# Where the pre-added weight sums of a Strassen-like feed-forward group begin, and when ScalarE splits its last lent operands

## Chip, cores, metric

The kernel runs on one core of a Trainium2 chip. The metric is device time in microseconds (us): the median of several executions. Engines: PE (TensorE), DVE (VectorE), ACT (ScalarE), POOL (GpSimd) and SP, which here only issues DMAs.

## The reference

One layer of a backbone on 640 tokens (128 context, 512 latent), width 1024: a half-step SwiGLU feed-forward block, a mixer (bidirectional chunked mLSTM beside a gated convolution), a second feed-forward block and a last norm, all in float32. What matters here is the second feed-forward block:

```python
D_MODEL, D_FF = 1024, 2816
def swiglu(h, w1, w2):
    a, b = jnp.split(h @ w1, 2, axis=-1)
    return (jax.nn.silu(a) * b) @ w2
...
    h = modulate(rmsnorm(x, norm_g[2]), sh2, sc2)
    x = x + 0.5 * g2[:, None, :] * swiglu(h, ffn2_w1, ffn2_w2)
...
y_prompt, y_sample = rmsnorm(xp, final_norm), rmsnorm(xs, final_norm)
```

## The kernel before

**Numbers.** Every float32 operand x is split into hi (rounded to the fp32r type; a ScalarE cast, line 75) and lo = x - hi (a VectorE subtraction, line 79). A product of two operands is three matmuls into the same accumulator: hi times hi, hi times lo, lo times hi (lines 288 to 290). Weight tiles are 128 x 512, hi named `wh`, lo named `wl`; the moving operand is 128 x 320, half of the 640 tokens.

**Pairs.** Work comes in pairs of 128-column weight tiles over 1024 rows (`pair_el`). A pair is computed as a 2 x 2 block product with seven block products instead of eight (a Strassen-Winograd form). In order: A11, S1, S2, A12, S3, S4, A22. S1 = A21 + A22, S2 = S1 - A11, S3 = A11 - A21 and S4 = A12 - S2 are sums of weight blocks (the code only adds; the signs go into the other operand and the last sums). Their partners are sums of the moving operand's blocks, in sets of four hi/lo tiles called 11, T1, T2, 21, T3, 22, T4 in the same order. A block product is 12 matmuls, a pair 84. PSUM tiles: `a` takes A11, is copied to `b` by ScalarE (line 332) and then takes A12; `b` takes S2, is copied to `c` by ScalarE (line 347, negated) and then takes S4; `c` takes S3 and A22. So the S3 product can't start before the copy of b to c is done. The steps are numbered 0 to 6, and a dictionary `at` names small functions that are emitted right behind a step; whatever is emitted earlier stands earlier in its engine's queue, and every engine works its queue in order.

**Weight sums.** In a pair that isn't `summed`, SP loads two 512 KB tiles (`wr`, line 218), and VectorE forms S1 to S4 into `ws` tiles (line 270; 128 x 512). In a `summed` pair, S1 and S3 come from the DMA: SP loads two 256 KB quarters into one `wr` tile, POOL issues two 256 KB loads that accumulate onto them (line 235), SP loads a 512 KB `wr` tile and a 256 KB `wq` tile. VectorE then makes only S2 and S4. `wr` has five buffers, `wq` one; the loads are issued in the program's order, as buffers come free, and the weight casts run four block products ahead of PE.

**Groups.** The second feed-forward block (`ffn` with groups 8, 8, 6) goes through the 2816 hidden columns in two groups of eight tiles (`eights`) and one plain group of six. The first two tiles of the first group are done elsewhere (`n_head` = 2). A group of eight has w1 pairs 0 to 7 (silu(a) times b, 1024 hidden columns in all), then four w2 pairs (m = 0, 2, 4, 6; the first of them `summed`) that multiply the result back to width 1024. In the w2 pairs the hidden activations take the place of the moving operand, again in seven sets: five in tiles of their own, T3 and T4 in tiles lent from the block's input. For that the input's T3 and T4 were stored to DRAM (`hd`); in the last w2 pair, behind steps 4 and 6, `h_back` has POOL issue eight loads each that bring them back (tiles `HT3h`, `HT3l`, `HT4h`, `HT4l`, line 1042). Behind step 4 of the next group's first pair, `x_end` has POOL issue the last two accumulating writes of the group's result to DRAM (`xd`, line 1030; the others were issued in the w2 pairs).

**Deferred steps.** The evaluations of a pair put the splits and subtractions that make the hidden sets into a list `lazy`: for pairs 0 to 3 three entries (split for set 11; a subtraction; split for T1), for pairs 4 to 7 three entries (T2; 21 and the last subtraction for T3; 22 and the addition for T4). They are filled behind step 0 of the next pair at the earliest. `relax` empties the list, `relax_some(n)` takes n entries. The second group's pairs empty it behind step 1 (`pops`); the first w2 pair empties it behind step 0, and then splits the last tile of T3 and the four of T4 (`put_lent`) behind steps 1 to 3.

Of the kernel before, what the change touches and what calls it, by code (L numbers as in the profile page):

```python
# [44 lines left out]
def mixer_step(ctx: ExitStack, tc: tile.TileContext, x_prompt, x_sample, state_C, state_n, state_m,  # L45
# [23 lines left out]
    def t3():  # L69
        return tp.tile([P, HT], F32, name="t3", bufs=8)  # L70
# [3 lines left out]
    def split(raw, hi, lo, owe=False):  # L74
        A.copy(hi, raw)  # L75
        if owe:
            owed.append(lambda: V.tensor_sub(lo, raw, f32(hi)))
        else:
            V.tensor_sub(lo, raw, f32(hi))  # L79
# [136 lines left out]
    def w_load(w, row0, nk, col0, ncol):  # L216
        def load(t):
            nc.sync.dma_start(t[:, :nk * P].rearrange("p (k n) -> p k n", k=nk),
                              dap(w, row0 * ncol + col0, [[ncol, P], [P * ncol, nk], [1, P]]))
        load.src = (w, row0, col0, ncol)  # L220
        return load
# [81 lines left out]
    def joined(a, b):  # L303
        return {i: [*a.get(i, ()), *b.get(i, ())] for i in {*a, *b}}

    def relax_some(n):
        for _ in range(min(n, len(lazy))):
            lazy.pop(0)()
# [66 lines left out]
    def pair_el(load1, load2, ev, e1=None, spare_v=False, acts=HB, at=None, calm=False, gated=None,  # L375
                summed=False):
        po = pair_ops(summed, e1)
        at = at or {}

        def emit():  # L380
            nf = len(fill)
            for i, _ in enumerate(pair_steps(ORDER, ev, spare_v, acts, gated)):
                if not calm:
                    relax(7 - i if i else 9)
                drain(nf - nf * (i + 1) // 7)
                for f in at.get(i, ()):
                    f()
        return dict(element(pair_loads(load1, load2, summed), [po[name] for name in ORDER], emit), pair=True)
# [91 lines left out]
    def blocks_of(p):  # L480
        return [(p[i], lambda h, ps, i=i: p[2](i, h, ps)) for i in range(2)]
# [86 lines left out]
    at = 0  # L568
# [288 lines left out]
    def upair():  # L857
        return (PO["u"].tile([P, HT], F32R, name="Uh", bufs=PO["un"]),
                PO["u"].tile([P, HT], F32R, name="Ul", bufs=PO["un"]))
# [4 lines left out]
    def hpair(o):  # L864
        return (hpool(o).tile([P, HT], F32R, name="H" + o + "h", bufs=4),
                hpool(o).tile([P, HT], F32R, name="H" + o + "l", bufs=4))
# [162 lines left out]
    def x_add(m, y):  # L1029
        G.dma_start(xd[m], y, accum_op=OP.add)  # L1030
# [7 lines left out]
    def h_back(o):  # L1038
        for k in range(4):
            HB[o][k] = hpair(o)  # L1040
            for i in range(2):
                G.dma_start(HB[o][k][i], hd[o, k, i])

    def eights(w1, w2, g, f0, n_head, head, more, back):

        spare = (*range(n_head, n_head + 4), 7) if f0 < n_head else (7,)
        UB = {o: [None] * 4 for o in OPS_H}

        def tile_of(m):
            if "xs" not in PO:  # L1050
                PO["xs"] = [xp.tile([P, T], (F32, F32R)[i // 4], name="x", bufs=KT) for i in range(KT)]
            return PO["xs"][m]
        slot = lambda a, k: tile_of(2 * a + k // 2)[:, hsl(k % 2)]
        raw3 = lambda k: slot(0, k)
        raw2 = lambda k: slot(1, k)

        def put_own(o, k, src):
            UB[o][k] = hl = upair()
            split(src, *hl)

        def put_22(k, src):
            UB["22"][k] = hl = [tile_of(4 + k)[:, hsl(i)] for i in range(2)]
            split(src, *hl)

        def put_lent(o, k, src):
            UB[o][k] = hl = hpair(o)
            split(src, *hl)

        def ev_of(j):
            sa, k = {}, j % 4  # L1070

            left = [lambda: put_own("11", k, sa[0])]
            diff_1 = [lambda: V.tensor_sub(raw2(k), raw3(k), sa[0]), lambda: put_own("T1", k, raw2(k))]

            def t2():
                V.tensor_sub(raw2(k), raw2(k), sa[1])
                put_own("T2", k, raw2(k))

            def t3_():
                put_own("21", k, sa[0])  # L1080
                V.tensor_sub(raw3(k), raw3(k), sa[1])

            def t4():
                put_22(k, sa[1])
                V.tensor_add(raw2(k), sa[0], raw2(k))
            diff_2 = [t2, t3_, t4]

            def ev(mi, h, src):
                if mi == 0:
                    sa[h] = raw3(k) if h and j < 4 else t3()  # L1090
                    A.activation(sa[h], src, AF.Silu)
                    return
                V.tensor_mul(sa[h], src, sa[h])
                if j < 4:
                    lazy.extend(diff_1 if h else left)
                elif h:
                    lazy.extend(diff_2)
            return ev
        grp = []
        for j in range(8):  # L1100
            p = (w_load(w1, 0, KT, (f0 + j) * P, 2 * DFF), w_load(w1, 0, KT, DFF + (f0 + j) * P, 2 * DFF), ev_of(j))
            at = {}
            if j == 7:
                lent = lambda k: lambda: put_lent("T3", k, raw3(k))
                at = {4: [lent(0), lent(1), lent(2)], 6: [flush]}
            due = j - n_head if f0 < n_head else 8
            if due:
                pops = {1: (3, 2, 1), 2: (2, 2, 2), 3: (3, 2)}.get(due, (8,))
                at = joined(at, {i + 1: [lambda n=n: relax_some(n)] for i, n in enumerate(pops)})
            if f0 + j < n_head:  # L1110
                head.extend(blocks_of(p))
            else:
                grp.append(pair_el(*p, at=joined(at, more.get(j, {})), spare_v=j in spare, calm=True,
                                   summed=j > 1))
        w2s = []
        PO["x_end"] = []
        for m in range(0, KT, 2):
            rows_ = lambda i, m=m: (tile_of((m + i) % 4), modT[:, g, m + i, 0:1])

            def ev(mi, h, src, m=m):  # L1120
                y = tile_of((m + mi) % 4)
                if h and m == KT - 2:
                    PO["x_end"].append(lambda: x_add(m + mi, y))
                    return
                if h:
                    x_add(m + mi, y)
                    return
                for a, b, cd in ((0, P, 1), (P, HT, 0)):
                    A.activation(y[:, a:b], src[:, a:b], AF.Copy, scale=modT[:, g, m + mi, cd:cd + 1])
            at = {}  # L1130
            if m == 0:
                four = lambda k: lambda: put_lent("T4", k, raw2(k))
                at = {0: [relax], 1: [lambda: put_lent("T3", 3, raw3(3)), four(0)], 2: [four(1)], 3: [four(2), four(3)]}
            elif m == KT - 2 and back:
                at = {4: [lambda: h_back("T3")], 6: [lambda: h_back("T4")]}
            w2s.append(pair_el(w_load(w2, f0 * P, 8, m * P, D), w_load(w2, f0 * P, 8, (m + 1) * P, D), ev,
                               acts=UB, at=at, gated=rows_, spare_v=m == 0, summed=m == 0))
        return grp, w2s

    def ffn(w1, w2, g, lists, head_of, n_head, e1=None, groups=(6, 6, 6, 4), more={}):  # L1140

        head, els, f0 = [], [], 0
        for gi, size in enumerate(groups):
            if size == 8:
                els.append(eights(w1, w2, g, f0, n_head, head, more.get(gi, {}), True))
                f0 += size
                continue
# [373 lines left out]
    def hsl(h):  # L1521
        return slice(*HALVES[h])
# [717 lines left out]
```

## Time and profile before

| What | us |
|---|---|
| median of 3 runs (lowest, highest) | 1654.85 (1653.64, 1657.85) |
| the profiled execution | 1655.89 |
| its span, first to last instruction | 1654.1 |
| PE busy in it | 1632.4 (99%) |
| DVE, ACT, POOL busy | 1281.4, 837.7, 257.0 |
| mean granted PE clock | 0.997 |

A row of a timeline gives start and duration in us, engine, line, operation, output<-input, and in brackets how long the engine had been idle before it and who ended that idle time. A row of waits gives the total, the number and the longest wait. "x<-y" uses the program's tile names, with buffer numbers left out. A DMA row of POOL is its issue; the time to landing is in the DMA view.

In the profiled execution, the second group's pair 0 begins at 1366.12, its pair 1 at 1384.71, pair 2 at about 1397.9. The first group's w2 pairs begin at 1315.55, the second group's at 1471.79.

### The profile page before, as it was taken

To read this page: it belongs to the slowest core of one execution; us is meant where nothing else is said; L and a number is where in the kernel's file an instruction comes from. 1 tells how busy PE (TensorE), PEld (TensorE's weight loads), DVE (VectorE), ACT (ScalarE), POOL (GpSimd) and SP (SyncE) were. 2 spreads that over 40 slices of the span, in tenths; PEclk is the share of its full clock that TensorE was granted. 3 is DMA by queue.
4 is the path that set the end of the run, shared out by engine and by line. 5 is a ranking of instruction groups with operands and counts; after the bars stand their busy time and mean duration, and the time that the engine had idled before them with its cause. 6 is when DMAs were issued, how large, how long until landed. Compare 5 with 4: busy or idle time off the path is not lost.

```text
span 1654.1 us, 29490 instructions
## 1 busy us (share of the span) xinstructions
PE 1632.4 (99%) x11093; PEld 1587.9 (96%) x11093; DVE 1281.4 (77%) x2710; ACT 837.7 (51%) x1841; POOL 257.0 (16%) x366
## 2 busy tenths in 40 slices
PE   8999999999999999999999999999999999999998
PEld 5999999999999999999999999999999998999997
DVE  6867877887778878788897788779688875786765
ACT  5642542543566655465561455632376664565543
POOL 2010000000031322121121222011123113213002
PEclk9999999999999999999999999999999999999999
DMA  9454343343353433342358333457378767768522
GB/s 322 114 164 120 106 126 112 103 128 92 113 179 93 113 89 91 85 119 68 93 184 255 106 90 80 114 170 220 107 185 194 162 127 149 159 139 195 168 80 64
DMA packets 305806, 222.46 MB, mean 134 GB/s; under 512 B 9971, under 2 KB 282746, under 8 KB 305664
## 3 DMA queue, kind: packets, MB, share of 16 engines
q1 hardware_dynamic: 270768, 162.03, 34.4%
q0 software_dynamic: 34864, 58.54, 15.3%
q8 instruction: 87, 1.43, 0.4%
q14 instruction: 55, 0.45, 0.1%
q10 hardware_dynamic: 32, 0.01, 0.0%
HBM read 194.75 MB, written 25.79 MB: 133 GB/s over the span
## 4 chain that ended last, share of the span: by engine, by line
PE 88%; ACT 3%; DVE 3%; DMA 3%; issue 1%; POOL 0%; SPq 0%; ACTq 0%; DVEq 0%; POOLq 0%
PE ps L288 27%; PE ps L289 27%; PE ps L290 27%; PE ax L1779 2%; PE ax L1810 2%; DMA wr<-in_ffn_w_dram 1%; PE ax L1782 1%; DVE wl L79 1%; ACT Uh L931 1%; ACT wh L75 1%; DMA early<-in_w_mod_dram 1%; PE ax L1756 1%; DMA xd<-x 0%; DMA HT3l<-hd 0%; DMA x<-rd 0%
## 5 line engine op out<-in xcount | busy, mean ns | idle before, releaser
L79 DVE TENSOR_TENSOR wl<-wr,wh 128x512 fp32r<-128x512 f32 (+1 forms) x403 | 273.8, 690 | 87.9 <-ACT wh L75 85.4
L75 ACT CAST wh<-wr 128x512 fp32r<-128x512 f32 (+1 forms) x405 | 236.8, 598 | 90.9 <-PE ps L289 72.7
L79 DVE TENSOR_TENSOR wl<-ws,wh 128x512 fp32r<-128x512 f32 x296 | 204.6, 691 | 57.4 <-ACT wh L75 56.7
L75 ACT CAST wh<-ws 128x512 fp32r<-128x512 f32 x296 | 181.2, 620 | 97.2 <-DVE ws L270 72.3
L288 PE MATMUL ps<-Uh,wh 128*128 128x320 f32 x576 | 179.6, 312 | 0.0
L289 PE MATMUL ps<-Ul,wh 128*128 128x320 f32 x576 | 177.9, 309 | 0.0
L290 PE MATMUL ps<-Uh,wl 128*128 128x320 f32 x576 | 177.7, 309 | 0.0
L288 PE MATMUL ps<-HT4h,wh 128*128 128x320 f32 x408 | 128.4, 315 | 0.0
L289 PE MATMUL ps<-HT4l,wh 128*128 128x320 f32 x408 | 126.2, 309 | 0.1
L290 PE MATMUL ps<-HT4h,wl 128*128 128x320 f32 x408 | 126.1, 309 | 0.0
L288 PE MATMUL ps<-H11h,wh 128*128 128x320 f32 x376 | 118.8, 316 | 0.5 <-ACT H11h L75 0.5
L288 PE MATMUL ps<-H21h,wh 128*128 128x320 f32 x376 | 117.7, 313 | 0.0
L289 PE MATMUL ps<-H11l,wh 128*128 128x320 f32 x376 | 116.5, 310 | 0.3
L290 PE MATMUL ps<-H21h,wl 128*128 128x320 f32 x376 | 116.3, 309 | 0.0
L290 PE MATMUL ps<-H11h,wl 128*128 128x320 f32 x376 | 116.1, 309 | 0.0
L289 PE MATMUL ps<-H21l,wh 128*128 128x320 f32 x376 | 116.1, 309 | 0.0
L288 PE MATMUL ps<-HT3h,wh 128*128 128x320 f32 x356 | 112.3, 316 | 3.8 <-ACT ps L347 2.2
L289 PE MATMUL ps<-HT3l,wh 128*128 128x320 f32 x356 | 110.7, 311 | 1.1 <-DMA HT3l<-hd 1.1
L290 PE MATMUL ps<-HT3h,wl 128*128 128x320 f32 x356 | 110.2, 309 | 0.0
L288 PEld LDWEIGHTS ps<-Uh,wh 128*128 128x128 f32 x576 | 108.1, 188 | 1.2 <-issue 0.8
L289 PEld LDWEIGHTS ps<-Ul,wh 128*128 128x128 f32 x576 | 108.1, 188 | 0.4 <-DVE Ul L79 0.4
L288 PE MATMUL ps<-H22h,wh 128*128 128x320 f32 x344 | 108.1, 314 | 0.0
(483 smaller groups left out, 4733.5 us busy)
## 6 DMA issues: line engine op xcount, KB each, us to landing
wr<-in_ffn_w_dram SPq DMA_DIRECT2D x88, 512.0 KB, 4.9
wr<-in_w_in_dram SPq DMA_DIRECT2D x72, 512.0 KB, 3.9
wr<-in_w_mod_dram SPq DMA_DIRECT2D x51, 512.0 KB, 4.0
wr<-in_ffn_w_dram SPq DMA_DIRECT2D x32, 384.0 KB, 3.4
wr<-in_ffn_w_dram SPq DMA_DIRECT2D x40, 256.0 KB, 4.4
xd<-x POOLq DMA_DIRECT2D x32, 320.0 KB, 5.9
wr<-in_ffn_w_dram POOLq DMA_DIRECT2D x28, 256.0 KB, 5.0
early<-in_w_mod_dram SPq DMA_DIRECT2D x13, 512.0 KB, 8.8
```

Of the source, the lines that this page charges most:

```text
L75: A.copy(hi, raw)
L79: V.tensor_sub(lo, raw, f32(hi))
L288: PE.matmul(ps, hi[:, ws], ah, start=start, stop=False, skip_group_check=True)
L289: PE.matmul(ps, hi[:, ws], al, start=False, stop=False, skip_group_check=True)
L290: PE.matmul(ps, lo[:, ws], ah, start=False, stop=stop, skip_group_check=True)
L931: A.activation(t[:, a:b], t[:, a:b], AF.Identity, scale=sc_, bias=bi_)
L1756: PE.matmul(p[:, :P], S["k", dt][:, sl], S["q", dt][:, sl], start=(dt == 0), stop=(dt == 1))
L1779: PE.matmul(p2[:, :DH + 1], S["q", dt][:, sl], S["C"][d][:, dt, :], start=(dt == 0), stop=(dt == 1))
L1782: PE.matmul(p1[:, :DH + 1], S["p", ch][:, d, :], PO["vt"][:, ch, :], start=True, stop=True)
L1810: PE.matmul(p[:, :DH + 1], kw[:, dt * P:(dt + 1) * P], PO["vt"][:, ch, :], start=True, stop=True)
```

## The change

Three edits in `eights`. First, in the second group (`f0` = 8, not below `n_head`) the pairs are `summed` from pair 4 on, not from pair 2; the first group stays as it was. Second, in pairs 0 to 4 of the second group only two of the deferred entries are taken behind step 1, the rest behind step 2, that is, behind ScalarE's copy of b to c in program order. Third, in the first w2 pair of both groups, two deferred entries are taken behind step 0, the rest behind step 1, and the splits for T3 and T4 are each emitted one step later.

```diff
             if due:
-                pops = {1: (3, 2, 1), 2: (2, 2, 2), 3: (3, 2)}.get(due, (8,))
+                pops = {1: (3, 2, 1), 2: (2, 2, 2), 3: (3, 2)}.get(due, (2, 8) if j < 5 else (8,))
                 at = joined(at, {i + 1: [lambda n=n: relax_some(n)] for i, n in enumerate(pops)})
             if f0 + j < n_head:
                 head.extend(blocks_of(p))
             else:
                 grp.append(pair_el(*p, at=joined(at, more.get(j, {})), spare_v=j in spare, calm=True,
-                                   summed=j > 1))
+                                   summed=j > (1 if f0 < n_head else 3)))
...
             if m == 0:
                 four = lambda k: lambda: put_lent("T4", k, raw2(k))
-                at = {0: [relax], 1: [lambda: put_lent("T3", 3, raw3(3)), four(0)], 2: [four(1)], 3: [four(2), four(3)]}
+                at = {0: [lambda: relax_some(2)], 1: [relax], 2: [lambda: put_lent("T3", 3, raw3(3)), four(0)],
+                      3: [four(1), four(2)], 4: [four(3)]}
```

## The prediction

> **What bounds the kernel now.** I read the page first, then the waits of the tensor engine in the stretch that the change touches (the second feed-forward block), then the busy times of single stages, then the timeline of the two or three places where the stages were too long. The page:
>
> ```profile
> span 1654.1 us, 29490 instructions
> PE 1632.4 (99%) x11093; PEld 1587.9 (96%) x11093; DVE 1281.4 (77%) x2710; ACT 837.7 (51%) x1841; POOL 257.0 (16%) x366
> ```
>
> PE is the bound, so only time in which PE waits, or issues slowly, can be won. Its waits between 1226 and 1560 us:
>
> ```profile
> PE ps L288 <- ACT ps L347: 2.2, 3, 0.8
> PE ps L288 <- DMA HT3h<-hd: 1.7, 4, 1.1
> PE ps L289 <- DMA HT3l<-hd: 1.1, 4, 0.4
> ```
>
> Three waits for ScalarE's copy of b to c (L347), eight for the T3 set that comes back from DRAM (hd). What they cost altogether is seen better in the stages, each one pair of column tiles with 84 matmuls:
>
> ```profile
> core 0: us, PE busy (x) PEld busy (x) DVE busy (x) ACT busy (x) POOL busy (x), PEclk, DMA share, GB/s
> 1315.55:1328.90 13.35, 12.57 (x85) 12.06 (x84) 11.94 (x26) 10.15 (x24) 0.00 (x0) 1.00 0.51 138
> 1366.12:1384.71 18.59, 15.82 (x86) 13.82 (x85) 7.63 (x14) 6.30 (x15) 12.45 (x21) 0.91 1.16 249
> 1384.71:1397.90 13.19, 12.61 (x87) 12.34 (x86) 8.90 (x17) 6.50 (x15) 1.59 (x2) 1.00 0.68 118
> 1397.90:1410.20 12.30, 12.30 (x85) 12.30 (x85) 8.81 (x17) 6.55 (x15) 0.56 (x1) 1.00 0.31 87
> 1471.79:1485.10 13.31, 12.52 (x84) 12.09 (x83) 11.82 (x25) 10.23 (x24) 0.00 (x0) 1.00 0.51 138
> 1521.00:1533.30 12.30, 12.30 (x86) 12.30 (x85) 8.01 (x14) 5.49 (x12) 10.25 (x19) 1.00 1.16 273
> ```
>
> The rows are: first w2 pair of the first group of eight; pairs 0, 1 and 2 of the second group; first w2 pair of the second group; first pair of the last group of six. An undisturbed pair takes 12.30 us, or 0.1465 us a matmul. Four of these stages are longer, by 1.05, 6.29, 0.89 and 1.01 us: 9.24 us, all that the touched stretch has to give.
>
> **The long stage.** PE and POOL in pair 0 of the second group, and the same place one group later:
>
> ```profile
> 1373.01 0.31 PE L290 MATMUL ps<-H21h,wl 128*128 128x320 f32 x1
> 1374.45 0.38 PE L288 MATMUL ps<-HT3h,wh 128*128 128x320 f32 x1 [1.13 <-DMA HT3h<-hd]
> ...
> 1380.09 0.47 PE L288 MATMUL ps<-H22h,wh 128*128 128x320 f32 x1
> ```
> ```profile
> 1364.58 2.63 POOL L235 DMA_DIRECT2D wr<-in_ffn_w_dram  x2 [6.60 <-DVE wl L79]
> 1366.10 1.68 POOL L1042 DMA_DIRECT2D HT3h<-hd  x1
> ...
> 1373.39 0.53 POOL L1042 DMA_DIRECT2D HT3l<-hd  x1 [2.41 <-DMA wr<-in_ffn_w_dram]
> ...
> 1381.18 1.31 POOL L235 DMA_DIRECT2D wr<-in_ffn_w_dram  x1 [1.03 <-DVE t L360]
> ...
> 1517.99 0.56 POOL L1042 DMA_DIRECT2D HT3h<-hd  x1 [3.77 <-PE ps L290]
> ...
> 1526.38 0.54 POOL L1042 DMA_DIRECT2D HT4l<-hd  x1
> ```
>
> Issues and median time to landing, from 1355 to 1390 us and then from 1505 to 1545:
>
> ```profile
> HT3h<-hd POOLq DMA_DIRECT2D x4, 160.0 KB, 8.6
> HT3l<-hd POOLq DMA_DIRECT2D x4, 160.0 KB, 8.5
> HT4h<-hd POOLq DMA_DIRECT2D x4, 160.0 KB, 5.6
> ```
> ```profile
> HT3l<-hd POOLq DMA_DIRECT2D x4, 160.0 KB, 4.1
> HT4h<-hd POOLq DMA_DIRECT2D x4, 160.0 KB, 6.1
> HT4l<-hd POOLq DMA_DIRECT2D x4, 160.0 KB, 6.2
> ```
>
>  In the second group two accumulating weight loads (pair 2's) stand in POOL's queue ahead of the 16 loads that bring T3 and T4 back. The first T3 load goes at 1366.10, each takes about 8.6 us to land, and the eighth waits 2.41 us for an accumulating load to land; it goes at 1373.39, when PE wants T3 at 1373.01 + 0.15 = 1373.16. The product on T3 ends at 1380.09 in place of 1374.92: 5.17 us. The other 1.12 us of the 6.29 are lost in the matmuls that follow, which go slower (0.47 us each in place of 0.31 at 1380.09; PEclk 0.91 for the stage). One group later no accumulating load is near. The stages lie 156.24 us apart, so 1517.99 stands for 1361.75, which is 4.35 us earlier than 1366.10; T3 lands in about 4 us, and the row of 1521.00 shows no loss.
>
> **The change part by part.** (1) Pairs 2 and 3 of the second group lose four accumulating loads on POOL (1.3 us of POOL each); SP issues two 512 KB loads a pair in place of four smaller ones. POOL's next accumulating loads are pair 4's, behind the two xd writes that follow T4. The 16 loads then see what they see in the last group. T3: last of eight issued near 1365.4, landed by 1369.5; needed from 1373.16. T4: last issued near 1370.1 (1526.38 - 156.24), landed by 1376.4; its last tile is needed at 1373.16 + 24 x 0.1465 + 10 x 0.1465 = 1378.1. Both in time, so the whole 6.29 us goes. Late next would be T4, with 1.7 us to spare.
>
> (2) In exchange VectorE makes two sums more in each of the two pairs:
>
> ```profile
> L270 DVE TENSOR_TENSOR ws<-wr x7: 681/684/685, 1383.5 to 1455.0; 128x512 f32<-128x512 f32 x7
> ```
>
> 4 x 0.684 = 2.74 us of DVE. In pair 2 it is busy 8.81 of 12.30 us, so 10.2 afterwards: hidden under PE, 0 on the path. Pair 1 of the same group already works so (8.90 busy) and its only loss is the copy. ScalarE's casts stay as many.
>
> (3) The small splits move behind L347. In the first w2 pair, ScalarE before:
>
> ```profile
> 1322.08 0.46 ACT L75 CAST HT3h<-x 128x320 fp32r<-128x320 f32 x1
> 1322.43 0.47 ACT L75 CAST HT4h<-x 128x320 fp32r<-128x320 f32 x1
> 1322.79 0.62 ACT L75 CAST wh<-wq 128x512 fp32r<-128x512 f32 x1
> 1323.31 0.43 ACT L347 ACTIVATE ps<-ps 128x320 f32<-128x320 f32 x1
> ```
> ```profile
> 1322.70 0.31 PE L290 MATMUL ps<-Uh,wl 128*128 128x320 f32 x1
> 1323.79 0.41 PE L288 MATMUL ps<-HT3h,wh 128*128 128x320 f32 x1 [0.78 <-ACT ps L347]
> ```
>
> Two lent casts (1322.08 to 1322.79, 0.71 us) leave the place ahead of L347; the cast of the 22 set moves too, from the step before to this one, but stays ahead of L347, at no gain. L347 starts at 1322.60, ends 1323.03, and PE starts near 1323.08 instead of 1323.79: 0.71 won, 0.23 of wait left (undisturbed: 1322.85). What is late next is T3's last tile, now cast behind L347: hi by 1323.5, lo on DVE 0.5 later, 1324.0; PE wants it at 1323.08 + 10 x 0.1465 = 1324.5. So it holds. Twice (both groups): 1.42 us. Bounds: 0 if ScalarE is held by something else, 1.05 + 1.01 = 2.06 if nothing is left.
>
> (4) In pair 1 of the second group ScalarE's cast for T1 stood ahead of L347 and waited for a DVE subtraction that waited for an xd write:
>
> ```profile
> 1390.60 0.49 DVE L1073 TENSOR_TENSOR x<-x,t 128x320 f32<-128x320 f32 x1 [0.87 <-DMA xd<-x]
> ```
>
> That cast now comes behind L347, and the xd write leaves POOL earlier too (it stood behind pair 3's accumulating loads): 0.89 us go. Between 0 and 0.89; I take all, since two independent edits remove it.
>
> **Sum.** 6.29 + 0.89 + 1.42 + 0 = 8.60 us off. The profiled execution took 1655.89 us (span 1654.1), so 1647.3 by its own time; the runs' median is 1654.85, 1.04 lower, so 1646.3 on that footing, in which all times below are given.
>
> **A rule weighed.** The long stage shows PEclk 0.91 although no wait in it is longer than 1.13 us. "TensorE: Matmul & The Clock Gate" of the Trainium skill (Part 1, the clock gate) says that the clock halves after an idle window of about 3.4 us; the trace has a slower clock with less idle than that. By the page any wait left in that stage would cost itself alone; by the rows it may cost up to 1.12 us more. If all waits go, both give the same sum; in the first rival they differ by that much.
>
> **The rivals.** First: the 16 loads still come late. They go at 1361.75 but land as slowly as before, since weights move at the same time (DMA share 1.16 in both stages). With 8.6 us each, T3's last lands at 1374.0, needed by 1374.6: in time. T4's loads go as T3's land (the eighth T3 load waited for the transfer eight issues back): 1370.35 to 1374.05, landing 5.6 to 8.6 later, the last at 1379.7 to 1382.7 against 1378.1. That keeps 1.5 to 4.5 us of wait and about 1.1 of slow clock; with 4.1 kept (the middle of both), 1650.4. Against it: the last group moves the same loads beside 273 GB/s without loss. 0.12.
>
> Second: the splits behind L347 don't help, as ScalarE has other work ahead (DVE hands it late data at these places), and the 1.42 stays: 1647.7; if pair 1 keeps its wait too, 1648.6. 0.12 for this, since the reordering is the least tested part.
>
> Third, on the other side: POOL's 16 issues get slow while DVE is busy. Before, DVE stood nearly still in that stage (7.63 of 18.59), and after the change it works on. If each issue waits out one DVE instruction of 0.68 us, 16 x (0.53 + 0.68) = 19.4 us pass until 1381.2, and T4 lands 6.2 later, 1387.4, 9.3 us too late, with 1.1 of slow clock: the gain of 8.6 is gone and 1656.7 results, slower by 1.8; another DVE instruction for each would make it far worse. It begins to cost when the 16 take over 10.1 us (1378.1 - 6.2 - 1361.75). In the last group they took 1526.38 - 1517.99 = 8.39 with DVE busy 8.01 of 12.30. 0.03. "SBUF — State Buffer" of the Trainium skill (section on the two separate sides) has such a rule: descriptors for POOL's DMAs aren't written while DVE holds the shared port; the 8.39 us in the last group don't show it for these instructions.
>
> Fourth: the change doesn't do what it says, and T3 waits for something ahead on POOL besides the accumulating loads, so only part (3) and (4) count: 1652.5. Against it: up to 1357 both groups' POOL issues repeat at 156.24 us, and the next entry ahead of T3 is the accumulating load. 0.03.
>
> **How the numbers follow.** Forecast 0.70 (its own range 1644.8 to 1648.0: 2.06 in place of 1.42, run to run 1 us); rivals 0.12, 0.12, 0.03, 0.03. A change under 0.3% (5.0 us here) can't be told from none. Faster by more: the forecast, the second rival and about a third of the first, with its milder end: 0.70 + 0.12 + 0.04 = 0.86; slower 0.02, as the third rival reaches past 0.3% only in its worse part; same 0.12. The range 1644.0 to 1651.0 takes in the second rival and the middle of the first.
>
> **What the profile after would show.** Right: the stage of pair 0 of the second group at 12.3 us, T3's first load 4.3 us earlier than before against pair 0's start, no PE wait on HT3 or HT4; the three L347 waits gone or under 0.3 us; pairs 2 and 3 with two more L270 sums each and still 12.3 us. Wrong: PE waits on HT4, a wait on HT3l L79 in the first w2 pairs, or pair 4's S1 late for its accumulating load.

## The result and the profile after

The changed kernel took 1647.85 us (median of 5 runs, 1647.20 to 1648.61), the one before 1654.85 (now also of 5 runs), so 7.0 us off by the medians. The ratio is 0.9954, 95% interval 0.994 to 0.9969, so 0.3 to 0.6% off. Its profiled execution took 1648.61 (span 1646.8), 7.28 less than the profiled one before. Forecast were 1646.3 and 8.6 us off, range 1644.0 to 1651.0.

The page after, and its waits of PE between 1226 and 1560 us, all of them:

```profile
span 1646.8 us, 29482 instructions
PE 1628.1 (99%) x11093; PEld 1585.3 (96%) x11093; DVE 1284.7 (78%) x2714; ACT 837.8 (51%) x1841; POOL 251.9 (15%) x362
```
```profile
PE ps L289 <- DVE HT4l L79: 0.5, 2, 0.3
```

The waits for the T3 transfers and for the copy at L347 are gone from this list; one wait is new. DVE works 3.3 us more, POOL has four instructions less. The stages after, first start, length, then busy times as before (first w2 pair of the first group; pairs 0, 1 and 2 of the second group; first w2 pair of the second group):

```profile
1316.09:1329.51 13.42, 13.09 (x87) 12.32 (x85) 11.84 (x25) 10.14 (x24) 0.00 (x0) 1.00 0.49 133
1366.45:1378.85 12.40, 12.40 (x87) 12.31 (x86) 7.66 (x14) 6.32 (x15) 5.97 (x10) 1.00 1.13 272
1378.85:1391.15 12.30, 12.30 (x87) 12.30 (x85) 9.78 (x19) 6.54 (x15) 2.59 (x2) 1.00 0.47 115
1391.15:1403.45 12.30, 12.30 (x86) 12.30 (x85) 9.87 (x19) 6.63 (x15) 2.63 (x3) 1.00 0.72 150
1464.99:1478.35 13.36, 13.03 (x87) 12.33 (x86) 11.77 (x24) 10.14 (x24) 0.00 (x0) 1.00 0.52 134
```

For the first w2 pairs the prediction's rows ended 0.3 us before the pair did, so the two pairs were 1.33 and 1.25 us over 12.30, not 1.05 and 1.01. From first matmul to first matmul of the next pair, before:

```profile
1315.55:1329.18 13.63, 12.85 (x87) 12.34 (x85) 12.22 (x26) 10.15 (x24) 0.00 (x0) 1.00 0.50 135
1471.87:1485.42 13.55, 12.76 (x86) 12.33 (x85) 12.14 (x25) 10.15 (x24) 0.00 (x0) 1.00 0.50 133
```

So pair 0 gave 18.59 - 12.40 = 6.19 us, pair 1 0.86 (13.16 by its first matmuls, 1384.71 to 1397.87; the prediction's row ends 0.03 later), and the two first w2 pairs 13.63 - 13.42 = 0.21 and 13.55 - 13.36 = 0.19: together 7.45, which is the difference of the profiled executions within 0.2 us. POOL in the long stage, after:

```profile
1362.08 0.56 POOL L1042 DMA_DIRECT2D HT3h<-hd  x1 [3.77 <-PE ps L290]
...
1366.84 0.59 POOL L1042 DMA_DIRECT2D HT4l<-hd  x1
1369.08 0.53 POOL L1042 DMA_DIRECT2D HT4h<-hd  x1 [1.65 <-DMA HT3h<-hd]
...
1371.67 0.59 POOL L1042 DMA_DIRECT2D HT4l<-hd  x1
1372.19 1.87 POOL L1030 DMA_DIRECT2D xd<-x  x2
1388.56 2.63 POOL L235 DMA_DIRECT2D wr<-in_ffn_w_dram  x2 [14.49 <-DVE t L360]
```

T3's first load goes 4.37 us ahead of pair 0's start (1366.45), where it went at 1366.10, 0.02 ahead of 1366.12, before. The T4 loads lose 1.65 us behind T3 loads that haven't landed: T3 took a median of 5.1 (hi) and 5.0 us (lo) to land, not the 4 that were forecast. T4's lo tiles in this stretch:

```profile
DMA to landing us min/median/max: 4.4/4.7/6.7
```

If the slowest is the last, issued at 1371.67, it lands at 1378.4, just as PE wants it (the matmul on it started at 1378.46 and was 0.09 us longer than the others): that is pair 0's last 0.1 us. The next accumulating loads come at 1388.56, behind the xd writes.

What was new shows in the first w2 pair (PE, then DVE):

```profile
1323.23 0.31 PE L290 MATMUL ps<-Uh,wl 128*128 128x320 f32 x1
1323.61 0.41 PE L288 MATMUL ps<-HT3h,wh 128*128 128x320 f32 x1
```
```profile
1328.55 0.31 PE L288 MATMUL ps<-HT4h,wh 128*128 128x320 f32 x1
1329.12 0.41 PE L289 MATMUL ps<-HT4l,wh 128*128 128x320 f32 x1 [0.26 <-DVE HT4l L79]
```
```profile
1328.17 0.49 DVE L323 TENSOR_TENSOR x<-t,t 128x320 f32<-128x320 f32 x1
1328.57 0.49 DVE L79 TENSOR_TENSOR HT4l<-x,HT4h 128x320 fp32r<-128x320 f32 x1
```

The gap ahead of T3 fell from 1.09 to 0.38 us (0.147 is undisturbed). But T4's last tile, split a step later, now has its lo part behind the gated sum (L323) in VectorE's queue (of T4's four splits the first, second and last moved by a step; the third stays behind step 3). That lo part is done at 1329.06 and PE wanted it at 1328.70. That gap of 0.57 and the slow matmul behind it take 0.53 of the 0.71 back.

### The profile page after: what moved, and what is told of

Its sections match the earlier page's. It is cut to its first block, busy times and chain, and to the rows that moved or that the text cites. A ratio compares the mean times of both kernels' runs of the same rounds, so it can differ in the third digit from the quotient of the medians.

```text
span 1646.8 us, 29482 instructions
## 1 busy us (share of the span) xinstructions
PE 1628.1 (99%) x11093; PEld 1585.3 (96%) x11093; DVE 1284.7 (78%) x2714; ACT 837.8 (51%) x1841; POOL 251.9 (15%) x362
## 4 chain that ended last, share of the span: by engine, by line
PE 89%; DVE 4%; ACT 3%; DMA 2%; issue 1%; SPq 1%; POOL 0%; ACTq 0%; DVEq 0%; POOLq 0%
PE ps L288 27%; PE ps L289 27%; PE ps L290 27%; PE ax L1780 2%; PE ax L1811 2%; DMA wr<-in_ffn_w_dram 1%; PE ax L1783 1%; DVE wl L79 1%; PE ax L1757 1%; ACT Uh L931 1%; ACT wh L75 1%; SPq L627 0%; DMA wl<-in_x_sample_dram 0%; DVE Uh L923 0%; PE ax L780 0%
## 5 line engine op out<-in xcount | busy, mean ns | idle before, releaser
L290 PEld LDWEIGHTS ps<-Uh,wl 128*128 128x128 f32 x576 | 108.1, 188 | 0.0
```

The source lines that it names most:

```text
L290: PE.matmul(ps, lo[:, ws], ah, start=False, stop=stop, skip_group_check=True)
```

## Experiments

The theory: order in POOL's queue makes the long stage; the copy of b to c in pair 1 waited, through VectorE, for the xd write. The rivals: the bytes moved beside the T3 loads; and, for the small waits, other causes than the order of the splits. First each edit alone, and POOL's order alone. Lengths of stages are from a pair's first matmul to the next pair's. Each ratio is to runs of the kernel before made beside the experiment (medians 1654.86 to 1655.36).

**The first edit alone.**

```diff
-                                   summed=j > 1))
+                                   summed=j > (1 if f0 < n_head else 3)))
```

> The kernel before with the first edit alone: pairs 2 and 3 of the second group not summed. Theory (the accumulating loads ahead of the T3 loads in POOL's queue cost the long stage, and through the late xd write also pair 1's wait for the copy): pair 0 of the second group 12.3 us instead of 18.59, pair 1 12.3 instead of 13.19, the two first w2 pairs unchanged at 13.35 and 13.31; 6.29 + 0.89 = 7.2 us off, about 1647.7. Rival (pair 1's wait comes from the order of the splits, whatever the xd write does): pair 1 stays at about 13.2, 6.3 us off, 1648.6.

Measured: 1647.96 us (ratio 0.9958, 0.9945 to 0.9971). Pairs 0 and 1 took 12.30 and 12.31 us, the first w2 pairs 13.63 and 13.55, as before. PE's waits in the stretch:

```profile
PE ps L288 <- ACT ps L347: 1.6, 2, 0.8
```

Two of the three L347 waits are left, those of the first w2 pairs. The theory held, pair 1 included: the first edit by itself brings all that a timing can tell.

**The second edit alone** (`pops` takes two entries, then the rest, in pairs 0 to 4 of the second group).

> The kernel before with the second edit alone: T1's split behind the copy of b to c in the second group's pairs 1 to 4. Theory (the copy stood behind a cast that waited for the xd write, so either remedy is enough): pair 0 stays at 18.6 us, pair 1 falls from 13.19 to 12.3 to 12.4 although its subtraction on line 1073 still waits for the xd write; 0.9 us off, about 1654. Rival (the copy is late for another reason): pair 1 stays at 13.2.

Measured: 1654.8 us (ratio 0.9997, 0.9988 to 1.0006). Pair 0 18.45, pair 1 12.31, L347 again with two waits. The lengths are as expected, but the reason isn't shown, because the subtraction on line 1073 did not wait for the xd write here:

```profile
1390.15 0.49 DVE L1073 TENSOR_TENSOR x<-x,t 128x320 f32<-128x320 f32 x1
```

In the run of the first edit alone, with the old order of splits and no such wait, L347 starts 1.40 us after line 1073 does. By that, an estimate, it would have started at 1391.55 here in the old order too and ended near 1391.97, before PE wants T3 at 1385.19 + 48 x 0.1465 = 1392.22. So pair 1 may have been short here without the edit. What the second edit does when the xd write is late is seen in the run with pair 3 summed, further down.

**The third edit alone** (the first w2 pairs' `at`).

> The kernel before with the third edit alone: the deferred steps in the first w2 pairs. Theory (the copy of b to c comes 0.71 us earlier, but T4's last tile, now split a step later, is late for A22 by about 0.53): the wait for L347 0.23 over the normal spacing instead of 0.94, a new wait of PE on HT4l before the tenth and eleventh matmul of A22, each first w2 pair about 13.1 to 13.2 us; 2 x (0.71 - 0.53) = 0.4 us off, within noise of 1654.85. Rival (the lateness of T4's last tile comes from something else, such as the other edits' DVE work): no wait on HT4l, 1.4 us off, about 1653.4.

Measured: 1655.5 us (ratio 1.0007, 0.9996 to 1.0017). The first w2 pairs took 13.44 and 13.34 us in place of 13.63 and 13.55, with the new wait:

```profile
PE ps L289 <- DVE HT4l L79: 0.5, 2, 0.3
```

So the new wait belongs to this edit and not to the DVE work that the others add. It wins 0.2 us a pair, too little for a timing.

**Same loads, other order: the accumulating loads of pair 2 behind T3 and T4.** A flag holds them back from step 0 of the last w2 pair until T4's loads are issued; PE, DVE, ACT and SP have the same instructions in the same order as before.

```diff
-        while accs and accs[0][0] <= n:
+        while accs and accs[0][0] <= n and not (ptr.get('wait') and n == 1 << 20):
...
-                at = {4: [lambda: h_back("T3")], 6: [lambda: h_back("T4")]}
+                at = {0: [lambda: ptr.update(wait=True)], 4: [lambda: h_back("T3")], 6: [lambda: h_back("T4"), lambda: ptr.update(wait=False)]}
```

> The kernel before, same loads and same sums, with one thing moved: pair 2's two accumulating loads are issued by POOL behind the 16 loads of T3 and T4 instead of ahead of them. Theory of the queue (order on POOL is what counts, not the bytes or the number of loads): T3's first load goes 4.3 us earlier against the stage and pair 0 takes 12.3 to 12.5 us; the xd writes now stand behind four accumulating loads and go near 13 us after pair 0's start, so pair 1's subtraction waits and pair 1 gets longer, 14 to 15 us; together 4.5 to 6 us off, 1649 to 1650.4. Rival of the bytes (T3 and T4 land late because of the weight bytes moved beside them, 1.25 MB a summed pair plus the accumulates against 1 MB): pair 0 stays above 15 us.

Measured: 1656.69 us (ratio 1.0008, 0.9998 to 1.0017): nothing won, although pair 0 is cured. Pairs 0 and 1:

```profile
1366.01:1378.31 12.30, 12.30 (x86) 12.30 (x85) 7.56 (x14) 6.22 (x15) 6.83 (x10) 1.00 1.15 268
1378.31:1398.70 20.39, 14.55 (x87) 14.28 (x85) 9.05 (x17) 6.53 (x15) 4.37 (x4) 0.83 0.63 105
```
```profile
1372.36 1.31 POOL L235 DMA_DIRECT2D wr<-in_ffn_w_dram  x1 [0.57 <-DMA HT4l<-hd]
1379.48 1.28 POOL L235 DMA_DIRECT2D wr<-in_ffn_w_dram  x1 [5.80 <-DMA wr<-in_ffn_w_dram]
1382.38 1.27 POOL L235 DMA_DIRECT2D wr<-in_ffn_w_dram  x1 [1.61 <-DMA wr<-in_ffn_w_dram]
1383.13 2.33 POOL L1030 DMA_DIRECT2D xd<-x  x2
```
```profile
1382.85 0.49 DVE L79 TENSOR_TENSOR Ul<-t,Uh 128x320 fp32r<-128x320 f32 x1 [0.85 <-ACT Uh L75]
1389.47 0.49 DVE L1073 TENSOR_TENSOR x<-x,t 128x320 f32<-128x320 f32 x1 [6.13 <-DMA xd<-x]
```

```profile
PE ps L288 <- ACT ps L347: 7.4, 3, 5.8
```

The rival of the bytes falls: pair 0 is at 12.30, and T3's hi tiles landed in a median of 3.8 us in place of 8.6, although the DMA moved as many bytes meanwhile (259 GB/s from 1361.60 to 1369.50, against 262 from 1366.10 to 1380.00 before). The DMA engines' busy share was lower (1.06 against 1.21), so whether the accumulating loads held T3 up by their place in the queue alone or also by the engine time of their own transfers isn't told apart; the edit takes them away from T3 in both ways. But the wait moved and grew. Pair 3's accumulating loads must wait for the plain loads onto the same tile, POOL stands still for 5.80 us, and the xd writes go at 1383.13, 17 us after pair 0's start where 13 were expected. VectorE then waits 6.13 us for them, ScalarE's cast for T1 behind it, the copy of b to c behind that, and PE 5.8 us for the copy.

**The same, behind the xd writes too.** The flag is released behind `x_end` of pair 0.

```diff
-    more = {... 1: {0: {4: [x_end]}}, 2: {0: {4: [x_end], ...
+    more = {... 1: {0: {4: [x_end, lambda: ptr.update(wait=False)]}}, 2: {0: {4: [x_end, lambda: ptr.update(wait=False)], ...
```

> The kernel before with the same loads, sums and splits; only POOL's order is changed: the accumulating loads of pairs 2 and 3 stand behind the T3 and T4 loads and behind the two xd writes. Theory of the queue: with nothing ahead of either, pair 0 takes 12.3 us and pair 1 12.3 us, although as many bytes are moved and summed as before; the first w2 pairs stay at 13.35 and 13.31; 7.2 us off, about 1647.7, the same as with pairs 2 and 3 not summed at all. Rival of the bytes: pair 1 or pair 2 gets longer, as the accumulating loads and the xd writes land more slowly together; then 2 us or more of it stay.

Measured: 1648.55 us (ratio 0.9958, 0.9945 to 0.997). Pairs 0 and 1:

```profile
1365.31:1377.61 12.30, 12.30 (x86) 12.30 (x85) 7.56 (x14) 6.22 (x15) 8.56 (x12) 1.00 1.16 275
1377.61:1389.92 12.31, 12.31 (x87) 12.31 (x85) 8.85 (x17) 6.57 (x15) 2.56 (x2) 1.00 1.00 162
```

All of the first edit's gain in these two pairs, with every accumulating load and every summed pair kept. What the first edit changes in bytes and sums is neither needed nor in the way; what counts is the order on POOL.

**One of the two pairs summed again, in the changed kernel.** `summed=j > (1 if f0 < n_head else 2)` keeps pair 3 summed, `summed=j > 1 and (f0 < n_head or j != 3)` keeps pair 2.

> The changed kernel, but pair 2 of the second group is summed again (pair 3 is not). POOL has pair 2's two accumulating loads ahead of T3, as before. Theory: the long stage is back, pair 0 at 16.5 to 18.6 us, pair 1 at 12.3, first w2 pairs as in the changed kernel: 1652 to 1654.5. Rival (the two summed pairs together, not their place in the queue, made the stage long): pair 0 under 15.5 us, 1651 or less.

> The changed kernel, but pair 3 of the second group is summed again (pair 2 is not). POOL then has pair 3's two accumulating loads between the T4 loads and the two xd writes, and nothing ahead of T3. Theory: pair 0 takes 12.3 us (pair 2's loads alone held T3 up); the xd writes go some 7 to 10 us later than in the changed kernel, the subtraction on line 1073 of pair 1 waits about 3 us for them, but as T1's split now stands behind the copy of b to c, PE has no wait for L347: the changed kernel's time, 1647 to 1648.5. Rival (a late xd write costs PE whatever stands behind the copy, since VectorE makes the weights' lo parts in the same queue): pair 1 or 2 longer by 1 us or more.

Measured with pair 2 summed: 1654.25 us (ratio 0.9996, 0.9987 to 1.0005), pair 0 at 17.98, pair 1 at 12.31, as the theory had it. With pair 3 summed: 1654.73 (ratio 0.9998, 0.9989 to 1.0008), pair 0 at 12.30, but pair 1 at 18.33 and pair 2 at 13.11; here the rival was right. The waits of PE and the instructions:

```profile
PE ps L288 <- DVE t L360: 4.3, 1, 4.3
```
```profile
1378.13 2.66 POOL L235 DMA_DIRECT2D wr<-in_ffn_w_dram  x2 [7.32 <-DVE t L367]
1379.67 2.92 POOL L1030 DMA_DIRECT2D xd<-x  x2
```
```profile
1389.38 0.49 DVE L1073 TENSOR_TENSOR x<-x,t 128x320 f32<-128x320 f32 x1 [5.57 <-DMA xd<-x]
```

There was no wait for L347 although line 1073 waited 5.57 us, so the second edit did what it does. But VectorE's queue stood still meanwhile, and the sum on line 360, which frees `c` for A22, came late behind it: PE waited 4.3 us there. By that, an estimate, some 5.57 - 4.3 = 1.3 us of a wait of line 1073 stay hidden under PE, more than the 0.87 us of the kernel before. Pair 2 lost its 0.81 without any wait, at a granted clock of 0.94. The profile puts the 7.32 us of POOL down to line 367, which ended at 1377.71; the plain loads onto the same tile were issued at 1371.89 and landed in a median of 5.8 us, at about the same time, so either may have ended it. One pair's two accumulating loads, in either place, cost about the whole gain: the losses don't add, they stand in for each other.

**Mending the new wait.** The changed kernel again and two other places for the splits in the first w2 pairs:

```diff
-                at = {0: [lambda: relax_some(2)], 1: [relax], 2: [lambda: put_lent("T3", 3, raw3(3)), four(0)],
-                      3: [four(1), four(2)], 4: [four(3)]}
+                at = {0: [lambda: relax_some(2)], 1: [relax], 2: [lambda: put_lent("T3", 3, raw3(3)), four(0)],
+                      3: [four(1), four(2), four(3)]}                                       # t4 early
+                at = {0: [lambda: relax_some(2)], 2: [lambda: put_lent("T3", 3, raw3(3)), relax, four(0)],
+                      3: [four(1), four(2), four(3)]}                                       # all behind
```

> The changed kernel once more, as the measure for the next two on the same chip: about 1647.5 to 1648; in each first w2 pair a gap of 0.38 us before the first matmul on HT3 and one of 0.57 before the eleventh on HT4, over a spacing of 0.147.

> The changed kernel with one step back: T4's last tile is split behind step 3 again, with T4's second and third. Theory (the step of one place made T4's last tile late): no gap on HT4l, the L347 gap stays at 0.38; 2 x 0.53 = 1.06 us less than the changed kernel, about 1646.7. Rival (T4's tile is late because ScalarE and VectorE are behind with their work at this point, whatever the order): the gap stays, or goes over to another wait, such as the weights of S4 or A22, and the time is that of the changed kernel.

> As the last one, and the deferred entry for set 22 as well as T3's last tile is emitted behind step 2, T3 first, so that only a weight cast stands between the two L340 copies and L347. Theory: L347 starts 0.35 us earlier, as soon as ScalarE has cast the weights, and PE finds it done; both gaps go, 2 x (0.53 + 0.33) = 1.7 us less than the changed kernel, about 1646. Rival: set 22's last tile becomes late for S4, a wait on the x tiles (L79) in its tenth matmul takes the place, and nothing is won over the kernel before it.

Measured: 1647.64, 1647.14 and 1646.68 us (ratios to before 0.9952, 0.9949, 0.9949, each within 0.0015). First w2 pairs: 13.42 and 13.36 in the changed kernel, 13.23 and 13.15, 13.23 and 13.16. Expected were gains of 0.53 and 0.86 a pair; both gave 0.2. The gap on HT4l went in both, and the L347 gap in the second, but A22 then waits at its start, here in the second:

```profile
1326.22 0.31 PE L290 MATMUL ps<-x,wl 128*128 128x320 f32 x1
1326.92 0.41 PE L288 MATMUL ps<-HT4h,wh 128*128 128x320 f32 x1 [0.39 <-ACT t L322]
```

L322 reads `c` before A22 may add to it, and stands behind the T4 casts on ScalarE. That is the rival of the expectation for T4's last tile alone: ScalarE is behind with its work (in the last version it has no idle time from 1319.64 to 1326.86, when L322 ends), and an order only chooses which product waits. The last version has the lowest median of all, but it is 0.96 us under the changed kernel's, and the ranges of the two overlap (1646.52 to 1647.59 and 1646.67 to 1648.07), so that it is faster isn't shown by the times.

**T4's last lo part on POOL**, its cast behind L322 (`four(3)` stands behind step 4 again; the diff leaves that line out):

```diff
-            split(src, *hl)
+            (A.copy(hl[0], src), G.tensor_sub(hl[1], src, f32(hl[0]))) if (o, k) == ("T4", 3) else split(src, *hl)
```

> As the kernel with set 22 and T3's last tile behind step 2, but T4's last tile is cast behind step 4 again, behind the gated copy L322 that holds A22 up there, and its lo part is subtracted by POOL (0.92 us for such a tile in the trace of before) instead of VectorE. Theory: L322 starts 0.36 us earlier and the gap before A22 falls from 0.70 to about 0.35; T4's last lo part comes about 1.0 us behind its cast, within 0.2 us of when PE wants it: 0.3 us better in each of the two pairs, 0.6 in all, about 1646.2, within the noise of one comparison but visible in the gaps. Rival: POOL's subtraction is later than that and the gap on HT4l returns, 0.4 us or more.

Measured: 1650.06 us (ratio 0.9972, 0.9961 to 0.9982), first w2 pairs 14.60 and 14.52. The gap before A22 fell to 0.33 as expected, but

```profile
1327.73 2.77 POOL L1067 TENSOR_TENSOR HT4l<-x,HT4h 128x320 fp32r<-128x320 f32 x1 [20.90 <-ACT HT4h L1067]
```
```profile
PE ps L289 <- POOL HT4l L1067: 2.9, 2, 1.5
```

The subtraction took 2.77 us, three times the 0.92 it was costed at, and lost 1.4 us a pair against the version before.

## Why the prediction was right, point by point

- **What bounds the kernel, and the long stage:** right. Both parts of the reading, the two accumulating loads ahead of T3 and the analogy one group later at 156.24 us, were borne out: T3's first load was forecast for 1361.75 and went at 1362.08, with the whole kernel 0.33 us later at that place. 6.29 forecast, 6.19 measured; the rest is 0.1 us at T4, which was named as next in line with 1.7 us to spare. T4's issues were held 1.65 us behind T3's, and with that the margin was gone.
- **Pairs 2 and 3, VectorE's four sums:** at no cost, as said; pair 2 went from 8.81 to 9.87 us of DVE in 12.30.
- **Pair 1:** 0.89 forecast, 0.86 measured. That "two independent edits remove it" is shown for the first edit by its run alone. For the second it isn't shown by its own run, in which the xd write was in time, but follows from the run with pair 3 summed, in which the copy did not wait for a much later xd write. What the prediction did not see is how much the order is worth in pair 1: pair 3's accumulating loads ahead of the xd writes are worth as much as pair 2's ahead of T3, for once T3 is in time they cost pair 1 some 6 us. The change is right to take both, not only pair 2's.
- **The first w2 pairs:** the step that failed. Forecast were 2 x 0.71 = 1.42, measured 0.40. The 0.71 at L347 came to the hundredth (gap 1.09 to 0.38, with the 0.23 that was to be left). But the prediction followed only T3's last tile behind the copy and not T4's last tile, which the same edit moves from step 3 to step 4, behind L323 on VectorE: minus 0.53 a pair. It stands in the diff: `four(3)` is the one entry that goes from 3 to 4. A wait of PE on HT4 was among the signs of being wrong that the prediction named, and this is where it came.
- **The rivals:** none came about in full. The first rival's mechanism is there on a small scale: T4's loads did wait for T3's to land, and it cost the 0.1 us above, not 4.1. POOL's issues did not get slow under a busy VectorE (eight T3 and two T4 loads from 1362.08 to 1366.84, 0.53 us apart, while DVE was busy 7.66 of 12.40). The second, that the 1.42 stays, is nearest to what happened, for another reason than it gave: its 1647.7 lies nearer to the measured 1647.85 than the forecast's 1646.3, but the copy at L347 did come 0.71 us earlier, so that nearness is luck. The slower clock after short waits, weighed in the prediction, came again in the run of the second edit alone: PEclk 0.81 in pair 0, with no wait of PE above 0.45 us. So in this kernel short waits close together go with a slower clock; how many it takes, no run separates. The long pair of the kernel with pair 2's loads behind T3 and T4 (PEclk 0.83) says nothing on this, for its slow clock followed a single wait of 5.84 us.

## What to carry to other kernels

A queue that works in order should be read as a list of who stands ahead of whom: in one run here an accumulating load waited 5.80 us for the plain load onto the same tile, and everything behind it waited with it, however small it was. Moving the offender a few places only moves the wait to the next thing behind it; put it behind all that PE will want soon, and check the next two waits in line before counting the gain. When splits are moved behind a critical copy, follow each of them to the product that uses it, on both engines: on an engine that is behind with its work, an order only chooses which product waits.

## What the hardware showed beyond that

POOL's subtraction of a 128 x 320 tile took 2.77 us, where 0.92 was the mean of an addition of that size (line 880) before. VectorE beside it ran its own two-input operations at their usual 0.68 us, but for the last, which took 0.89. "SBUF — State Buffer" of the Trainium skill (section on the two separate sides) says that POOL and a VectorE operation with two SBUF inputs exclude each other at a shared port; a POOL operation that takes three times as long agrees with it. So does the kernel before, where a VectorE subtraction of line 79 took 1.08 us in place of 0.68 beside a POOL sum of 1.35. But no run here separates the port from other causes: line 880 writes plain float32, this subtraction the rounded type.

The long stage varied from run to run with the same queue order: pair 0 took 18.59, 18.45 and 17.06 us in three kernels that have the same instructions up to there on POOL (before, the second edit alone, the third alone), at a granted clock of 0.91, 0.81 and 0.90.
